# Decode attention: rotary keys gathered feature-first, and all scores of a half batch in one burst

## The chip, the cores and the metric

The kernel runs on one core of a Trainium2 chip. The metric is the device time of one execution in microseconds (us), lower is better. The kernel before takes 1249.53 us, the median of 3 runs (1249.14 to 1250.53). The engines are named as the profile names them: PE is TensorE's matmul (PEld its weight loads), DVE is VectorE, ACT is ScalarE, POOL is GpSimd, SP is SyncE, which here issues DMAs.

## The reference

One layer of a hybrid decoder is computed for a prompt of 512 tokens and for 8 sampled sequences of 4 tokens each, with shared weights in float32: a SwiGLU feed-forward network (FFN), a mixer of a gated linear recurrence (HGRN2) and latent attention (MLA) side by side, and a second FFN. The part that the change touches is the attention of the sampled tokens over their past of 4096 positions, which lie in a cache of pages of 128 rows, found through a page table:

```python
past_c = cache_kv_latent[l][page_table].reshape(Bs, past_len, KV_LORA)   # 256 latent features
past_r = cache_k_rope[l][page_table].reshape(Bs, past_len, QK_ROPE)      # 64 rotary features
...
s = (einsum('bqhr,bsr->bhqs', ql, c_kv) + einsum('bqhd,bsd->bhqs', qr, k_rope)) * scale
p = softmax(s, axis=-1)
return einsum('bhqs,bsr->bqhr', p, c_kv)
```

Each sequence has 4 tokens x 4 heads = 16 queries. A score is a product over 256 latent and 64 rotary features; the value product reads the same latent rows again. The host may lay out inputs beforehand; both kernels use that for weights, and the changed one for the rotary cache too.

## The kernel before, in words

The program is one stream of instructions written by Python and placed on the engines in an order that follows the source with small shifts. It has these stages: the first FFN over all tokens (to about 395 us in the profile), the recurrence, the prompt's attention with the output projection of the first half of the prompt, then the **decode stage** (`decode`, L1437), in which the attention of the sampled tokens over the cache runs interleaved with the second FFN of the first half of the prompt (`gb`, the generator `ffn`, L324), and at last the rest of that FFN and the second half of the tokens.

In the decode stage two generators are stepped in turn (L1517 to L1528): 94 steps of `decode`, with 100 steps of `gb` spread evenly among them. A step of `gb` is a few dozen FFN matmuls: gate and up products (L277) with their sigmoid work on ACT and DVE, or down products (L288 and L259). Their weights come by DMA from SP into `wraw`, and each tile is split in a rounded part `wh` on ACT (L250) and the rest `wl` on DVE (L251).

The past of a sequence is split in two halves of 2048 positions: 16 objects `Half` (L1352), each with two blocks of 1024 positions. A block is a tile of 128 partitions with 8 rows each.

- `gather` (L1360) fetches a block of latent rows (8 KB per partition) by an indirect DMA on POOL into one of seven slots (`ulb`, `uhb`, `ha`, `hb`, `mb`, `q0`, which the profile shows as `q`, and `dx`).
- `gather_r` (L1369) does the same for the rotary rows of both blocks of a half: two indirect DMAs of 2 KB per partition into `rraw`, which has two buffers.
- `turn` (L1376): scores need the features on the partitions. A DVE transpose of 32x32 blocks turns 64 features of a block into `kh`. A half takes five steps (`JS`, L65): the rotary features (8, 9) first, then the latent ones two by two; each step is two transposes of 128x512, one per block. `kh` has four buffers.
- `score` (L1384) multiplies a step's `kh` with the queries `qbd` on PE: 16 matmuls of 64 partitions x 32 queries x 128 positions, which run side by side on parts of the array (in the trace an instruction takes 269 ns and they start about 14 ns apart). The five steps accumulate in two PSUM banks. Which steps are multiplied where is set by `RUNS` (L68): steps 0 to 2 (48 matmuls) at step 2 of the five steps of a cycle, steps 3 and 4 (32 matmuls) at step 4. Then the scores are copied to SBUF (L1399, ACT and DVE) and their maximum is taken (L1401). `qsplit` (L1247) prepares the queries of the next sequence.
- `peak` (L1403), one cycle later: the maximum is spread with a matmul `pm` (L1405), reduced on DVE (L1407, L1410), the exponential is taken on ACT (L1411), transposed on DVE (`pt`, L1413) and copied into `pbuf` (L1417, 12 copies on ACT and 4 on DVE).
- `value` (L1419), at step 4 of that cycle and right behind the scores of the next half: 16 matmuls of `pbuf` with the latent blocks as they were gathered (L1426). Then the freed slots are gathered anew.

In the trace every float32 matmul stands as two instructions, so 48 matmuls are x96; a row of the instruction order counts matmuls.

The loop that sets this order:

```python
for st in range(len(JS)):
    if at(2):
        for k in RUNS.get(st, ()):
            at(2).score(k)
...
    if n > 1 or n == 1 and st >= 1:
        if n != 2 or st >= 2:
            turn(at(2).top if at(2) and st == len(JS) - 1 else None)
```

`at(k)` is the half whose gathers began k cycles ago, and `turn(top)` queues the next transpose on DVE, with `top` behind the maximum of the scores. The gather of the next half's rotary rows is issued with the first transpose of a half (L1452), once `rraw` has been turned.

## Time and profile before

| what | value |
|---|---|
| timed runs | 1249.14, 1249.53 and 1250.53 us, median 1249.53 |
| profiled execution, first to last instruction (span) | 1241.4 us |
| its mean granted TensorE clock | 0.999 |
| PE busy | 1215.0 us (98%) |
| DVE busy | 982.7 us (79%) |
| ACT busy | 738.8 us (60%) |
| POOL busy | 76.5 us (6%) |
| first score transpose to last value product of the stage | 707.3 to about 951 us |

The profiled execution has no other time than its span; 8.1 us lie between the span and the median of the timed runs. Busy time is the union of an engine's instructions, and the ends of matmuls are modelled, so PE can lose time between two starts without showing as idle. In a row of the timeline there stand the start, the length, the engine, the source line, the operation, the tile written and those read, the count, and in brackets the idle time of the engine before it and what ended that. In a row of the chain of waits there stand start, length, engine, tile and line.

### The profile page before, as it was taken

To read this page: it belongs to the slowest core of one execution; us is meant where nothing else is said; L and a number is where in the kernel's file an instruction comes from. 1 tells how busy PE (TensorE), PEld (TensorE's weight loads), DVE (VectorE), ACT (ScalarE), POOL (GpSimd) and SP (SyncE) were. 2 spreads that over 40 slices of the span, in tenths; PEclk is the share of its full clock that TensorE was granted. 3 is DMA by queue.
4 is the path that set the end of the run, shared out by engine and by line. 5 is a ranking of instruction groups with operands and counts; after the bars stand their busy time and mean duration, and the time that the engine had idled before them with its cause. 6 is when DMAs were issued, how large, how long until landed. Compare 5 with 4: busy or idle time off the path is not lost.

```text
span 1241.4 us, 29997 instructions
## 1 busy us (share of the span) xinstructions
PE 1215.0 (98%) x12366; PEld 1151.3 (93%) x12366; DVE 982.7 (79%) x1976; ACT 738.8 (60%) x1559; POOL 76.5 (6%) x80
## 2 busy tenths in 40 slices
PE   8999999999999999999999999999999999999997
PEld 6999999999999989988898888888888999999997
DVE  7897788878678888786877899999998778566665
ACT  7675545455366744545758766666656776554455
POOL 0000000000000000000001312322310000000000
PEclk9999999999999999999999999999999999999999
DMA  6232333232264213333233868878776635545451
GB/s 238 86 115 90 103 103 102 86 99 91 62 221 147 82 54 105 88 94 130 85 105 117 339 214 303 310 282 323 258 275 232 198 106 188 184 137 188 150 151 60
DMA packets 73113, 195.59 MB, mean 158 GB/s; under 512 B 12336, under 2 KB 27728, under 8 KB 68240
## 3 DMA queue, kind: packets, MB, share of 16 engines
q1 hardware_dynamic: 64512, 150.47, 37.3%
q0 software_dynamic: 7168, 41.95, 9.2%
q8 instruction: 97, 1.59, 0.5%
q10 hardware_dynamic: 1296, 1.26, 0.3%
q14 instruction: 40, 0.33, 0.1%
HBM read 183.97 MB, written 9.67 MB: 156 GB/s over the span
## 4 chain that ended last, share of the span: by engine, by line
PE 79%; DVE 11%; ACT 7%; issue 2%; DMA 2%; SPq 0%; DVEq 0%; ACTq 0%
PE acc L259 29%; PE acc L277 13%; PE dn L259 8%; PE Y L575 7%; PE X L575 4%; PE Z L575 4%; DVE kh L1381 3%; PE acc L731 3%; DVE wl L251 2%; ACT wh L250 1%; PE s L1393 1%; ACT pbuf L1417 1%; DMA wraw<-w_g 1%; PE pa L952 1%; PE o L1426 1%
## 5 line engine op out<-in xcount | busy, mean ns | idle before, releaser
L250 ACT CAST wh<-wraw 128x1024 fp32r<-128x1024 f32 (+2 forms) x194 | 185.0, 957 | 164.3 <-PE acc L259 103.7
L251 DVE TENSOR_TENSOR wl<-wraw,wh 128x1024 fp32r<-128x1024 f32 (+2 forms) x194 | 214.6, 1108 | 72.2 <-ACT wh L250 71.6
L277 PE MATMUL acc<-uha,wh 128*128 128x256 f32 (+1 forms) x528 | 155.5, 295 | 0.1
L277 PE MATMUL acc<-uha,wl 128*128 128x256 f32 (+1 forms) x528 | 150.0, 285 | 0.8 <-DVE wl L251 0.7
L277 PE MATMUL acc<-ula,wh 128*128 128x256 f32 (+1 forms) x528 | 150.5, 286 | 0.0
L259 PE MATMUL acc<-uhb,wh 128*128 128x288 f32 (+1 forms) x432 | 128.0, 296 | 0.0
L259 PE MATMUL acc<-uhb,wl 128*128 128x288 f32 (+1 forms) x432 | 127.0, 295 | 1.0 <-DVE wl L251 0.8
L259 PE MATMUL acc<-ulb,wh 128*128 128x288 f32 (+1 forms) x432 | 127.5, 295 | 0.0
L277 PEld LDWEIGHTS acc<-uha,wh 128*128 128x128 f32 x528 | 99.2, 188 | 8.8 <-issue 7.9
L277 PEld LDWEIGHTS acc<-uha,wl 128*128 128x128 f32 x528 | 99.2, 188 | 2.3 <-DVE wl L251 1.6
L277 PEld LDWEIGHTS acc<-ula,wh 128*128 128x128 f32 x528 | 99.4, 188 | 1.6 <-issue 1.2
L259 PEld LDWEIGHTS acc<-uhb,wl 128*128 128x128 f32 x432 | 81.2, 188 | 1.6 <-DVE wl L251 1.6
L259 PEld LDWEIGHTS acc<-uhb,wh 128*128 128x128 f32 x432 | 81.0, 187 | 0.2 <-ACT uhb L170 0.2
L259 PEld LDWEIGHTS acc<-ulb,wh 128*128 128x128 f32 x432 | 81.1, 188 | 0.1
L259 PE MATMUL dn<-hh,dh 128*128 128x272 f32 x256 | 74.3, 290 | 0.0
L259 PE MATMUL dn<-hh,dl 128*128 128x272 f32 x256 | 73.7, 288 | 0.0
L259 PE MATMUL dn<-hl,dh 128*128 128x272 f32 x256 | 73.6, 288 | 0.0
L277 PE MATMUL acc<-uhb,wh 128*128 128x272 f32 x176 | 52.8, 300 | 0.0
L1417 ACT COPY pbuf<-pt 32x64 f32<-32x64 f32 x192 | 46.5, 242 | 10.1 <-DVE pt L1413 7.3
L259 PE MATMUL acc<-hlb,wh 128*128 128x288 f32 x176 | 52.1, 298 | 0.0
L259 PE MATMUL acc<-hhb,wh 128*128 128x288 f32 x176 | 51.8, 298 | 0.0
L1393 PE MATMUL s<-kh,q 64*32 64x128 f32 x2560 | 48.0, 273 | 3.5 <-DVE kh L1381 3.5
(632 smaller groups left out, 3881.3 us busy)
## 6 DMA issues: line engine op xcount, KB each, us to landing
wraw<-w_u SPq DMA_DIRECT2D x66, 512.0 KB, 4.3
wraw<-w_g SPq DMA_DIRECT2D x65, 512.0 KB, 3.9
wraw<-w_d SPq DMA_DIRECT2D x40, 384.0 KB, 3.5
wraw<-w_in SPq DMA_DIRECT2D x24, 512.0 KB, 3.5
wraw<-w_d SPq DMA_DIRECT2D x32, 320.0 KB, 3.1
wraw<-w_d SPq DMA_DIRECT2D x16, 512.0 KB, 3.8
wraw<-w_o SPq DMA_DIRECT2D x16, 512.0 KB, 3.7
g_S<-state SPq DMA_DIRECT2D x4, 512.0 KB, 4.4
```

Source lines behind the costliest of these rows:

```text
L250: nc.scalar.copy(wh[:, :kt], w[:, :kt])
L251: nc.vector.tensor_tensor(wl[:, :kt], w[:, :kt], f32(wh[:, :kt]), op=ALU.subtract)
L259: nc.tensor.matmul(out, a, b, start=n == 0, stop=n == last)
L277: nc.tensor.matmul(acc[:, :n], a[:, k], b[:, k], start=k + i == 0, stop=k == kt - 1 and i == 2)
L575: nc.tensor.matmul(bank, a[p][:, k], b[q][:, k], start=first and k + n == 0, stop=k == 3 and n == 2, skip_group_check=True)
L731: nc.tensor.matmul(accs[x, d], wts[d][p][:, k], hs[k // 2][q][:, k % 2, x], start=k + n == 0, stop=k == nf - 1 and n == 2)
L952: nc.tensor.matmul(po[es, c].rearrange("p (n m) -> p n m", m=m), kx[:, cs], up(qx[:, cs], m), start=True, stop=True, skip_group_check=True)
L1381: nc.vector.transpose(kh[:, g].rearrange("p a j k -> p a (j k)"), src)
L1393: nc.tensor.matmul(self.s[r][c * 32 : c * 32 + 32, :P], q[rs, j], kh, start=st + jj == 0, stop=st == len(JS) - 1 and jj == 1, skip_group_c ...
L1417: (nc.scalar.copy if g else nc.vector.tensor_copy)(self.p[g * 32 : g * 32 + 32, c // 2, c % 2 * 4 : c % 2 * 4 + 4, self.i * 16 : self.i * ...
L1426: nc.tensor.matmul(o[g : g + 32, :R], self.p[:, c, a], self.craw[c][:, a], start=i + c == 0 and a < 4, stop=i + c == 2 and a >= 4, skip_gr ...
```

## The change

The rotary cache is laid out by the host so that, within a page, a feature's values for all positions lie together (features 0 to 31 as rows, and in each row the two halves of the features, the row number within the group of 8, and 16 positions). `gather_r` then brings rows that are already turned: four indirect DMAs of 1 KB per partition for a half, with an index tile `idr` of their own, into `rk` (two buffers, one per block). The five transposes of a half become four; a step of rotary scores reads `rk` directly, in runs of 16 values. The rotary features are now the last step.

`score` makes all 80 matmuls of a half at step 4 of the cycle (`RUN`), right ahead of the value products. `TURNS` sets two transposing steps at step 0 and one each at steps 1 and 2 of the same cycle; the first waits for the maximum of the scores before. The query split of the next sequence stands behind the maximum. The index tile takes two small loads on SP (`pr_sb`, `p32`) and one DVE operation in `decode_prep`. The numbers of steps of `decode` and `gb` stay 94 and 100.

```diff
-JS = ((8, 9), (0, 1), (2, 3), (4, 5), (6, 7))
+JS = ((0, 1), (2, 3), (4, 5), (6, 7), (8, 9))
 KHB = 4
-PEAK = 1
-RUNS = {2: (0, 1, 2), 4: (3, 4)}
+STEPS = 5
+PEAK, RUN = 1, 4
+TURNS = (2, 1, 1, 0, 0)
...
             def decode_prep():
+                pr_sb = mk([P, 2 * NBLK], I32, "pr_sb")
+                nc.sync.dma_start(pr_sb, ptr)
+                p32 = mk([P, 1], F32, "p32")
+                nc.sync.dma_start(p32, cf[:, C_P32 : C_P32 + 1])
+                nc.vector.tensor_scalar(out=idr, in0=pr_sb, scalar1=float(RD // 2), scalar2=p32, op0=ALU.mult, op1=ALU.add)
...
             def gather_r(self):
                 for blk in (2 * self.n, 2 * self.n + 1):
-                    rraw = mk([P, ROWS, RD], F32, "rraw", 2)
-                    off = bass.IndirectOffsetOnAxis(ap=idx[:, blk : blk + 1], axis=0)
-                    nc.gpsimd.indirect_dma_start(rraw.rearrange("p a r -> p (a r)"), None, pool_r, off)
-                    self.rraw.append(rraw)
+                    rk = mk([P, 2, 2, ROWS, 16], F32, "rk", 2)
+                    for i in range(2):
+                        off = bass.IndirectOffsetOnAxis(ap=idr[:, 2 * blk + i : 2 * blk + i + 1], axis=0)
+                        nc.gpsimd.indirect_dma_start(rk[:, i].rearrange("p j a k -> p (j a k)"), None, pool_r, off)
+                    self.rk.append(rk)
...
-            def score(self, st):
+            def score(self):
                 q = qbd[self.b % 2]
-                if st == 0:
-                    self.s = [ps("s", own=True) for _ in range(2)]
-                for jj, j in enumerate(JS[st]):
-                    for c in range(4):
-                        for r in range(2):
-                            rs = slice(r * 64, r * 64 + 64)
-                            kh = self.kh[st][rs, c // 2, c % 2 * 4 : c % 2 * 4 + 4, jj]
-                            nc.tensor.matmul(self.s[r][c * 32 : c * 32 + 32, :P], q[rs, j], kh, start=st + jj == 0, stop=st == len(JS) - 1 and jj == 1, skip_group_check=True)
-                if st == 1 and self.i and self.b + 1 < NB:
-                    qsplit(self.b + 1)
-                if st < len(JS) - 1:
-                    return
+                self.s = [ps("s", own=True) for _ in range(2)]
+                for st, js in enumerate(JS):
+                    for jj, j in enumerate(js):
+                        for c in range(4):
+                            for r in range(2):
+                                rs = slice(r * 64, r * 64 + 64)
+                                as_ = slice(c % 2 * 4, c % 2 * 4 + 4)
+                                if j < 8:
+                                    kh = self.kh[st][rs, c // 2, as_, jj]
+                                    out = self.s[r][c * 32 : c * 32 + 32, :P]
+                                else:
+                                    kh = self.rk[c // 2][rs, :, jj, as_].rearrange("p i a k -> p a i k")
+                                    out = self.s[r][c * 32 : c * 32 + 32, :P].rearrange("p (a i k) -> p a i k", a=4, i=2)
+                                nc.tensor.matmul(out, q[rs, j], kh, start=st + jj == 0, stop=st == len(JS) - 1 and jj == 1, skip_group_check=True)
...
                 self.top = nc.vector.tensor_reduce(self.mx, self.e, axis=AX.X, op=ALU.max)
+                if self.i and self.b + 1 < NB:
+                    qsplit(self.b + 1)
...
-            ups = [(h_, st) for h_ in H for st in range(len(JS))]
+            ups = [(h_, st) for h_ in H for st in range(len(JS) - 1)]
...
-                    if st == 0 and h_.n + 1 < NH2:
-                        H[h_.n + 1].gather_r()
...
-                for st in range(len(JS)):
-                    if at(2):
-                        for k in RUNS.get(st, ()):
-                            at(2).score(k)
+                for st in range(STEPS):
+                    if st == RUN and at(2):
+                        at(2).score()
                     if n < 3 and st == 0:
-                        if n == 0:
-                            H[0].gather_r()
                         gather(2 + n // 2)
+                    if st == 0 and 0 <= n - 1 < NH2:
+                        at(1).gather_r()
...
-                    if n > 1 or n == 1 and st >= 1:
-                        if n != 2 or st >= 2:
-                            turn(at(2).top if at(2) and st == len(JS) - 1 else None)
+                    if n > 1:
+                        for i in range(TURNS[st]):
+                            turn(at(3).top if at(3) and st + i == 0 else None)
...
-        "pool_r": g["cache_k_rope"].reshape(-1, ROWS * RD),
+        "pool_r": np.ascontiguousarray(g["cache_k_rope"].reshape(-1, 16, ROWS, 2, 32).transpose(0, 4, 3, 2, 1)).reshape(-1, 16 * ROWS * 2),
...
+        "ptr": np.ascontiguousarray(np.repeat(g["page_table"].reshape(NBLK, 4, 2), 32, axis=1).transpose(1, 0, 2)).reshape(P, 2 * NBLK),
```

## The prediction

> **What bounds the kernel now.** I read the slices of the page first, to find the stage that the change touches, then the busy time by stretches. Columns: stretch, length, then PE, weight loads (PEld), DVE, ACT and POOL busy with instruction counts, granted clock, DMA share, GB/s.

> ```profile
> 707.00:754.00 47.00, 44.65 (x777) 39.65 (x779) 45.85 (x97) 29.69 (x70) 8.97 (x9) 1.00 0.73 265
> 754.00:798.00 44.00, 44.00 (x803) 39.40 (x807) 39.85 (x84) 28.37 (x76) 13.28 (x12) 1.00 0.90 321
> 798.00:839.00 41.00, 39.58 (x802) 33.90 (x785) 38.87 (x89) 26.46 (x74) 12.81 (x12) 1.00 0.77 270
> 839.00:884.00 45.00, 44.86 (x848) 40.10 (x854) 43.02 (x94) 27.25 (x72) 11.98 (x12) 1.00 0.86 313
> 884.00:941.00 57.00, 56.56 (x1114) 48.87 (x1100) 52.98 (x121) 35.00 (x97) 11.91 (x11) 1.00 0.69 241
> 941.00:1241.00 300.00, 290.78 (x2222) 285.67 (x2214) 202.39 (x337) 177.41 (x322) 1.35 (x1) 0.99 0.51 159
> ```

> The decode stage is the first five rows, 234 us. TensorE is busy 229.65 of them and VectorE 220.57 (the sums of their columns): two engines stand close to full, so PE time saved counts only while DVE follows. The clock is full and DMA is not the limit except for stretches at 0.90. The last row is untouched by the change.

> Next, the chain of waits through that stage, in order of time (start, length, what).

> ```profile
> 752.61 0.68 DVE kh L1381
> 753.33 0.64 PE s L1393 x24
> 753.97 1.86 PE o L1426 x32
> ...
> 794.53 3.04 PE acc L277 x24
> ...
> 848.90 1.52 PE s L1393 x96
> 850.42 4.46 PE acc L259 x36
> 854.88 1.09 PE s L1393 x64
> 855.97 1.86 PE o L1426 x32
> ```

> PE alternates between FFN pieces and two score bursts per half batch, and in places a score burst stands behind a DVE transpose (first two rows). Each matmul counts as two instructions here: 48 score matmuls are x96, 32 are x64. The waits of the stage (total us, times, longest):

> ```profile
> POOL rraw L1373 <- DVE kh L1381: 133.3, 16, 13.3
> ...
> PEld s L1393 <- DVE kh L1381: 5.4, 7, 1.7
> ...
> PE s L1393 <- DVE kh L1381: 3.5, 7, 1.4
> ```

> What one such wait looks like on PE:

> ```profile
> 836.77 0.67 PE L1393 MATMUL s<-kh,q 64*32 64x128 f32 x32
> 838.54 0.42 PE L1393 MATMUL s<-kh,q 64*32 64x128 f32 x8 [1.11 <-DVE kh L1381]
> 839.14 0.64 PE L1393 MATMUL s<-kh,q 64*32 64x128 f32 x24 [0.17 <-DVE kh L1381]
> 839.71 1.07 PE L1426 MATMUL o<-ulb,pbuf 128*32 128x256 f32 x16
> ```

> The x64 burst takes 839.71 - 836.77 = 2.94 us instead of 1.09: 1.85 lost, of which 1.28 show as PE idle. So the 3.5 us of idle understate the loss; the 5.4 us of the weight loads are nearer, since 3.5 x 1.85/1.28 = 5.1.

> **The change, part by part.** *Bursts merged.* From the chain: 32 more score instructions cost 1.52 - 1.09 = 0.43 us, 0.0134 each; one burst of 160 would take 1.09 + 96 x 0.0134 = 2.38 us where the two take 2.61: 0.23 saved. An FFN piece costs (4.46 - 3.04)/12 = 0.118 us per matmul, so x24 holds 3.04 - 24 x 0.118 = 0.20 us that does not scale, paid at each break; one break less saves it. Together 0.43 us of pure PE time per half batch. The first of the 16 halves is broken up otherwise, so 15 x 0.43 = 6.5 us, on the path as long as PE is.

> *Score waits on transposes.* Now all transposes of a half are queued early in its cycle and the burst stands at its end, so the 5.4 us should go. Bounds: 3.5 (PE's idle alone) and 8.9 (both rows added, as if they never overlapped).

> *Rotary transposes removed.*

> ```profile
> L1381 DVE STREAM_TRANSPOSE kh<-rraw 128x512 f32<-128x512 f32 x32 | 20.4, 675 | 0.0
> ```

> 20.4 us of DVE work go, 1.3 per half. PE hides them except for the waits already counted, so they are worth nothing by themselves; they give DVE room to keep up with a PE that is 4% faster: 220.57 - 20.4 = 200.2 us in about 224, 89%.

> *What comes next: softmax to value.* In gate/up halves the value products stand right behind another chain, shown for one half, from the end of its scores (first row) to its value products (last):

> ```profile
> 810.84 0.64 PE L1393 MATMUL s<-kh,q 64*32 64x128 f32 x24 [0.28 <-DVE kh L1381]
> ...
> 815.04 0.42 DVE L1401 TENSOR_REDUCE mxh<-q 128x1 f32<-128x256 f32 x1
> ...
> 819.30 1.18 DVE L251 TENSOR_TENSOR wl<-wraw,wh 128x1024 fp32r<-128x1024 f32 x1
> ...
> 820.74 0.28 DVE L1407 TENSOR_REDUCE q<-pm 128x16 f32<-128x128 f32 x1
> ...
> 821.34 0.51 ACT L1411 ACTIVATE q<-q,mbd 128x256 f32<-128x256 f32 x1 [1.18 <-DVE mq L1410]
> ...
> 822.63 0.44 DVE L1413 STREAM_TRANSPOSE pt<-q 128x256 f32<-128x256 f32 x1
> ...
> 823.27 3.07 ACT L1417 COPY pbuf<-pt 32x64 f32<-32x64 f32 x12
> ...
> 825.27 1.29 DVE L1381 STREAM_TRANSPOSE kh<-rraw 128x512 f32<-128x512 f32 x2
> ...
> 825.67 1.07 PE L1426 MATMUL o<-q,pbuf 128*32 128x256 f32 x16
> ```

> Probabilities are complete at 823.27 + 3.07 = 826.34, 0.7 us after the value products began (these need the last of them only in their second half). So this chain, 14.9 us from the scores' end at 811.48, has no slack today. It is made of DVE queueing: 3.6 us until the maximum starts, 7.6 from there to the transpose `pt`. In the changed order two transposes (0.6 us each by the spacing of such rows) come ahead of `pt` and two weight subtractions (about 1.15 each, the 819.30 row) go behind it: 1.1 us less; and 1.3 us per half less queue ahead of the maximum. I take 12 to 12.5 us. It stands against cycles, from one half's value products to the next, of 11.8 (the shortest I find, 14.04 us between the 825.67 and 839.71 rows less 1.85 of wait and 0.43) to 13.8 (811.48 to 825.67 less 0.43): a wait of under 1 us in some halves, 1.0 us in all; bounds 0 and 5.4, all that the other wait gave.

> *Rotary gathers.* 64 of them replace 32, and with two buffers those of the next half can only start when the burst has read the last; a latent gather queues behind four instead of two.

> ```profile
> 811.65 0.95 POOL L1373 DMA_INDIRECT rraw<-pool_r,idx  x1 [7.29 <-DVE kh L1381]
> 812.90 0.95 POOL L1373 DMA_INDIRECT rraw<-pool_r,idx  x1 [0.30 <-issue]
> 814.16 0.95 POOL L1366 DMA_INDIRECT hb<-pool_c,idx  x1 [0.31 <-issue]
> ...
> 827.50 1.51 POOL L1373 DMA_INDIRECT rraw<-pool_r,idx  x1 [0.30 <-issue]
> ```

> Their landing (minimum, median, maximum from issue), first of `rraw`, then of the latent gathers, in this stage:

> ```profile
> DMA to landing us min/median/max: 3.3/4.6/6.8
> ```

> ```profile
> DMA to landing us min/median/max: 6.2/8.5/10.9
> ```

> Pitch 1.25 us. The fourth rotary gather starts 0.2 + 3 x 1.25 = 4.0 us after the burst and lands at 7.3 to 10.8; the next burst reaches its rotary part 0.45 us before its end (32 instructions), at 11.8 - 0.45 = 11.3 or later. Covered. The latent gather starts at 811.65 + 5.0 = 816.65 instead of 814.16. Its first reader in this case:

> ```profile
> 830.12 0.67 DVE L1381 STREAM_TRANSPOSE kh<-hb 128x512 f32<-128x512 f32 x1
> ```

> Today 830.12 - 814.16 - 8.5 = 7.5 us of slack. Of that 2.5 go to the queue and 2 to 4 to the shorter cycle and the earlier maximum: 1 to 3 are left at the median landing, none at 10.9. A late one stops DVE and all behind it, the softmax chain above first. I charge 0.5 us, bounds 0 and 4. Bytes are the same, so the DMA share rises only by the shorter stage.

> *Rotary scores.* 16 of the 80 matmuls read runs of 16 floats instead of 32. No row shows such a read. Nearest are the `kh` rows at 0.0134 us per instruction; the other end is twice that, 32 x 0.0134 = 0.43 us per half, 6.9 in all. I take 0, since the element count is the same. [...] No trace of before can show it.

> *Small edits.* Two small loads on SP and one DVE operation of 64 elements ahead of the stage: 0.2 us, bounds 0 and 4.6 if DVE had to wait for a landing. The query split moves behind the maximum; its copies are the same: 0.

> How the order moves. PE, one half in the gate/up part, `s` scores, `o` value products, `acc` FFN. Before:

> ```order
> L277 MATMUL acc<-ula,wh 128x256
> L277 MATMUL acc<-uha,wl 128x256
> L1393 MATMUL s<-kh,q_8192 32x128 x32
> L1426 MATMUL o<-q_8787,pbuf 32x256 x8
> L1426 MATMUL o<-dx,pbuf 32x256 x8
> L277 MATMUL acc<-uha,wh 128x256
> ```

> and now:

> ```order
> L280 MATMUL acc<-uha,wl 128x256
> L1409 MATMUL s<-kh,q_8193 32x128 x64
> L1409 MATMUL s<-rk,q_8193 32x128 x16
> L1440 MATMUL o<-q_8793,pbuf 32x256 x8
> L1440 MATMUL o<-dx,pbuf 32x256 x8
> L280 MATMUL acc<-uha,wh 128x256
> ```

> The 48 that stood alone in the FFN are now in front of the value products. DVE at the end of the same half, `pt` to the copy of the next scores. Before:

> ```order
> L1413 STREAM_TRANSPOSE pt<-q_8192 128x256
> L1381 STREAM_TRANSPOSE kh<-ulb 128x512
> L1417 COPY pbuf<-pt 32x4x16 x4
> L1381 STREAM_TRANSPOSE kh<-uhb 128x512
> L336 TENSOR_TENSOR sil<-sil,sit 128x256
> L1381 STREAM_TRANSPOSE kh<-rraw 128x512 x2
> L365 TENSOR_TENSOR sil<-sil,acc 128x256
> L251 TENSOR_TENSOR wl<-wraw,wh 128x768
> ```

> and now:

> ```order
> L1427 STREAM_TRANSPOSE pt<-q_8193 128x256
> L254 TENSOR_TENSOR wl<-wraw,wh 128x1024
> L1431 COPY pbuf<-pt 32x4x16 x4
> L254 TENSOR_TENSOR wl<-wraw,wh 128x1024
> L254 TENSOR_TENSOR wl<-wraw,wh 128x768
> L339 TENSOR_TENSOR sil<-sil,sit 128x256
> ```

> No transpose for the scores stands behind `pt` any more; weight work has moved there. POOL in the same part, `rraw` and `rk` rotary gathers, the rest latent ones. Before:

> ```order
> L1373 DMA rraw<-pool_r,idx 128x512 x2
> L1366 DMA hb<-pool_c,idx 128x2048
> L1366 DMA mb<-pool_c,idx 128x2048
> L1373 DMA rraw<-pool_r,idx 128x512 x2
> L1366 DMA q_8787<-pool_c,idx 128x2048
> ```

> and now:

> ```order
> L1383 DMA rk<-pool_r,idr 128x256 x4
> L1375 DMA hb<-pool_c,idx 128x2048
> L1375 DMA mb<-pool_c,idx 128x2048
> L1383 DMA rk<-pool_r,idr 128x256 x4
> L1375 DMA q_8793<-pool_c,idx 128x2048
> ```

> The latent gathers keep their places, each pair behind four.

> **The sum.** The profiled span is 1241.4 us, the median of the timed runs 1249.5; I keep the 8.1 us between them. -6.5 (bursts) -5.4 (waits) +1.0 (softmax) +0.5 (gathers) +0.2 = -10.2: **1239.3 us**, a span near 1231.

> **Rivals.**
> *Softmax takes the place of the transposes.* PE gets faster, the value products wait for `pbuf`, and the 5.4 us come back there. For: no slack today. Against: DVE loses 1.3 us per half on that very chain. 1249.5 - 6.5 + 0 to 2: 1243 to 1245.
> *Short runs at half pace.* The 6.9 us are paid on PE: 1239.3 + 6.9 = 1246.2. Against: the same number of elements.
> *Slower: the rotary gather becomes the cycle.* Burst end, four gathers, landing, burst: if the fourth landed later than about 9.4 us from its issue (past about 10.1 the whole gain is gone), a cycle of 13.8 us (102.0 us for 7 halves between the 753.97 and 855.97 rows, less 0.43 and 0.36 of waits) could not hold it (13.8 - 0.45 - 4.0). At the latent gathers' worst, 10.9, each half loses 1.5 us more, 22 in all: 1239.3 + 22 = 1261. For: four in a row cannot be started ahead. Against: 6.8 at worst today, 2.6 short of the point. [...]
> *More.* The start of the stage, where the scores stood in five pieces, gives 2 to 4 us more: 1236. That the change doesn't do what it says is excluded by the order.

> **Chances.** The forecast 0.60 (its own range 1236.5 to 1242); more 0.05; softmax 0.18; half pace 0.09; gather 0.08. A measurement of this kernel tells about 0.2%, 2.5 us, from no change. Faster: 0.60 + 0.05 + 0.18 + a third of half pace 0.03 = 0.86; same: the rest of half pace, 0.06; slower 0.08. The range leaves out half pace, the gather case and the tip of "more", 0.20 in all: 1234.5 to 1245.

> **What would show it.** Right: 160 score instructions in one piece of about 2.4 us without a break, PE not waiting for `kh`, no `kh<-rraw`, DVE about 200 us in a stage of about 224. Wrong: value products (`o`) or DVE transposes that wait (for `pbuf`, for a latent gather), a break inside the burst ahead of `rk`, or the last x32 of a burst longer than 0.43 us.

## The result, and the profile after

| | median | runs | against before in the same sitting |
|---|---|---|---|
| new kernel | 1261.38 us | 1254.59 to 1267.29 (6) | before 1250.36 us; ratio 1.0084, interval 1.0060 to 1.0108 |
| new kernel, once more (e14) | 1262.68 us | 1260.66 to 1265.76 (4) | before 1250.03 us; ratio 1.0099, interval 1.0077 to 1.0122 |

The kernel is slower by 0.8 to 1.0%, some 11 us, where 1239.3 us (0.8% faster) was forecast. The result lies outside the range and on the other side.

First the same stretches of the profile after as were read before (columns as there):

```profile
754.00:798.00 44.00, 40.69 (x678) 37.40 (x679) 34.15 (x75) 24.89 (x68) 15.34 (x16) 0.96 0.86 304
798.00:839.00 41.00, 36.40 (x723) 31.45 (x707) 33.60 (x76) 23.97 (x66) 18.44 (x18) 0.96 0.75 253
```

VectorE is down as forecast (34.15 us where it was 39.85), but TensorE is no longer full: 40.69 of 44 us and 36.40 of 41, with 678 matmuls where there were 803. The clock is 0.96 instead of 1.00. The last value products of the stage tell where the loss lies. They start here in the new kernel:

```profile
965.95 1.41 PE L1440 MATMUL o<-hb,pbuf 128*32 128x256 f32 x16
```

and here in the kernel before:

```profile
950.17 1.41 PE L1426 MATMUL o<-hb,pbuf 128*32 128x256 f32 x16
```

That is 15.8 us later, and the spans of the two profiles differ by 1257.5 - 1241.4 = 16.1: all of it is in the decode stage. The medians differ by 11.0 us only, since the first profile of before is of a quicker execution than its timed runs (e12 below). What TensorE waits for there (total us, times, longest):

```profile
PEld o L1440 <- issue: 12.9, 17, 3.0
...
PE o L1440 <- issue: 7.9, 5, 2.5
...
PEld o L1440 <- ACT pbuf L1431: 6.8, 11, 1.5
...
PEld s L1409 <- issue: 4.5, 2, 2.3
...
PE s L1409 <- issue: 4.0, 2, 2.0
```

No row has a wait of the scores for `kh` any more: that part came as forecast. In its place stand long waits with "issue", which means that the profile shows nothing that was waited for. Two of them in the timeline of TensorE, and between them a score burst that runs through to its value products (that half breaks one value product later, at 802.65; the view starts at 781, so its first row lacks the burst's first 8 instructions):

```profile
780.77 1.90 PE L1409 MATMUL s<-kh,q 64*32 64x128 f32 x120
782.41 0.76 PE L1409 MATMUL s<-rk,q 64*32 64x128 f32 x32
783.10 1.07 PE L1440 MATMUL o<-dx,pbuf 128*32 128x256 f32 x16
783.99 0.61 PE L1440 MATMUL o<-ulb,pbuf 128*32 128x256 f32 x7
787.07 0.95 PE L1440 MATMUL o<-ulb,pbuf 128*32 128x256 f32 x9 [2.47 <-issue]
...
797.31 2.03 PE L1409 MATMUL s<-kh,q 64*32 64x128 f32 x128
799.08 0.74 PE L1409 MATMUL s<-rk,q 64*32 64x128 f32 x32
799.76 1.07 PE L1440 MATMUL o<-uhb,pbuf 128*32 128x256 f32 x16
...
827.98 0.74 PE L1409 MATMUL s<-rk,q 64*32 64x128 f32 x31
830.67 0.29 PE L1409 MATMUL s<-rk,q 64*32 64x128 f32 x1 [1.95 <-issue]
```

The two breaks come in the midst of a row of equal matmuls, whose operands the ones before had read already. The page's list of DMA queues has one that led on:

```profile
q8 instruction: 97, 1.59, 0.5%
```

97 packets of 16 KB, 1.59 MB. The trace has 24,964 instructions of TensorE, counting the weight load of each matmul (a score burst of 160 and the 32 value products behind it make 384, in 2.45 us, from 797.31 to 799.76, and 1.86 us). 1.59 MB over 24,964 are 64 bytes each, so a packet holds 256, and 97.5 such blocks fit the 97 packets; in e8 below, 2048 more instructions bring 8 more packets. So I counted the place of each break among TensorE's instructions in the trace, and took from the trace when the last packet before it had landed. These are all breaks over 1.4 us in the stage, from the start of the matmul before (time of the end in us, length, place among TensorE's instructions, place modulo 256, time since the last packet landed):

```
787.07  2.85  14530  194  1.39
802.65  2.01  15042  194  1.35
830.67  2.22  16066  194  1.50
846.34  2.27  16577  193  1.42
940.41  1.46  19906  194  1.41
955.34  2.25  20418  194  1.43
```

Every one falls on the same place modulo 256 (which place it is depends on where the count starts), and ends 1.35 to 1.50 us after a packet has landed. This looks as if TensorE had used up its instructions; e2, e3 and e8 test it.

### The profile page after: what moved, and what is told of

It reads as the page before. It is cut to its first block, busy times and chain, and to the rows that moved or that the text cites. A ratio compares the mean times of both kernels' runs of the same rounds, so it can differ in the third digit from the quotient of the medians.

```text
span 1257.5 us, 30075 instructions
## 1 busy us (share of the span) xinstructions
PE 1217.1 (97%) x12366; PEld 1155.1 (92%) x12366; DVE 965.2 (77%) x1945; ACT 739.1 (59%) x1559; POOL 105.2 (8%) x112
## 3 DMA queue, kind: packets, MB, share of 16 engines
q8 instruction: 97, 1.59, 0.5%
## 4 chain that ended last, share of the span: by engine, by line
PE 85%; ACT 7%; DVE 5%; issue 2%; DMA 0%; SPq 0%; DVEq 0%; another core or an unknown queue 0%; ACTq 0%
PE acc L262 30%; PE acc L280 17%; PE dn L262 8%; PE Y L578 6%; PE X L578 4%; PE Z L578 4%; PE acc L734 3%; PE s L1409 2%; PE o L1440 2%; ACT wh L253 2%; DVE kh L1391 1%; ACT pbuf L1431 1%; PE pa L956 1%; PE s L1206 1%; DVE wl L254 1%
## 5 line engine op out<-in xcount | busy, mean ns | idle before, releaser
L254 DVE TENSOR_TENSOR wl<-wraw,wh 128x1024 fp32r<-128x1024 f32 (+2 forms) x194 | 214.8, 1110 | 81.6 <-ACT wh L253 75.7
L280 PE MATMUL acc<-uha,wh 128*128 128x256 f32 (+1 forms) x528 | 155.5, 295 | 0.7 <-issue 0.7
L280 PE MATMUL acc<-ula,wh 128*128 128x256 f32 (+1 forms) x528 | 151.8, 288 | 0.0
L280 PE MATMUL acc<-uha,wl 128*128 128x256 f32 (+1 forms) x528 | 151.3, 287 | 0.3 <-issue 0.2
L280 PEld LDWEIGHTS acc<-uha,wh 128*128 128x128 f32 x528 | 100.5, 191 | 8.2 <-issue 7.6
L280 PEld LDWEIGHTS acc<-ula,wh 128*128 128x128 f32 x528 | 100.6, 191 | 1.5 <-issue 1.2
L280 PEld LDWEIGHTS acc<-uha,wl 128*128 128x128 f32 x528 | 100.5, 190 | 1.5 <-issue 0.9
L1383 POOL DMA_INDIRECT rk<-pool_r,idr x64 | 67.2, 1051 | 147.5 <-PE s L1409 124.5
L280 PE MATMUL acc<-uhb,wh 128*128 128x272 f32 x176 | 52.8, 300 | 0.0
L262 PE MATMUL acc<-hhb,wl 128*128 128x288 f32 x176 | 51.4, 294 | 0.0
```

Of the source, the lines that this page charges most:

```text
L254: nc.vector.tensor_tensor(wl[:, :kt], w[:, :kt], f32(wh[:, :kt]), op=ALU.subtract)
L262: nc.tensor.matmul(out, a, b, start=n == 0, stop=n == last)
L280: nc.tensor.matmul(acc[:, :n], a[:, k], b[:, k], start=k + i == 0, stop=k == kt - 1 and i == 2)
L1383: nc.gpsimd.indirect_dma_start(rk[:, i].rearrange("p j a k -> p (j a k)"), None, pool_r, off)
```

## The experiments

Three theories were tested. **F** (fetch): TensorE's instructions come in blocks of 256. The next block is there 4 to 6 us after the current one is entered (in the six rows above 4.0 to 5.7 us lie between the entry and the end of the break), and the joined run of 384 dense instructions uses one up faster (384 in 2.45 + 1.86 us, so 256 in some 2.9). **G**: the rotary gathers. First meant as gathers or rotary rows that come late; after e1 as G2: many gathers in a row disturb TensorE. **S**: the value products wait for the probabilities.

The runs fell on several chips, on which the kernel before takes 1250 to 1252 us, and on one (e9, e10) 1244; so ratios to before in the same sitting are compared. A ratio to before still holds what the two gathers of before cost on that chip: e1 to e4 ran on one chip, e5 to e8 on a second, e9 and e10 on a third, e11 to e14 on a fourth. The table has each run's ratio with its interval. Then follow, worked out from the starts of successive matmuls in the decode stage, the time over a bound (0.03 us in scores, 0.07 in value products, 0.215 in FFN, where the usual spacing is 0.014, 0.06 on average and 0.12): at block boundaries (place 190 to 197 modulo 256), elsewhere in scores and elsewhere in FFN. These sums move by up to about 1 us with the bound. The column "half clock" is the time in the stage with a granted clock of 0.50. The last column is the time from the first score matmul to the last value product. The 3.6 us in scores of the kernel before are its waits for `kh`.

| run | ratio (interval) | boundary | scores | FFN | half clock | stage |
|---|---|---|---|---|---|---|
| before, first profile | 1 | 3.2 | 3.6 | 0 | 0 | 239.5 |
| before, e12 | 1 (1250.44 us, one run) | 2.8 | 8.2 | 0 | 0 | 246.2 |
| new, first profile | 1.0084 (1.0060-1.0108) | 15.3 | 0 | 4.8 | 6.8 | 254.9 |
| new, e14 | 1.0099 (1.0077-1.0122) | 15.2 | 0 | 8.5 | 10.2 | 258.8 |
| e1 new, cut burst | 1.0156 (1.0131-1.0182) | 5.3 | 8.1 | 12.7 | 6.8 | 266.0 |
| e2 new, 64 more instructions | 1.0158 (1.0131-1.0185) | 21.4 | 0 | 8.3 | 17.1 | 266.8 |
| e3 new, 192 more | 1.0099 (1.0063-1.0136) | 12.6 | 0 | 4.6 | 6.8 | 255.2 |
| e4 new, no rotary gather | 0.9990 (0.9978-1.0002) | 10.6 | 0 | 1.9 | 0 | 242.5 |
| e5 before, four rotary gathers | 1.0259 (1.0240-1.0278) | 2.2 | 24.4 | 1.6 | 17.1 | 281.0 |
| e6 cut burst, no rotary gather | 0.9930 (0.9911-0.9950) | 3.3 | 2.3 | 0 | 0 | 238.8 |
| e7 before, no rotary gather | 0.9933 (0.9915-0.9951) | 3.0 | 3.9 | 0 | 0 | 239.6 |
| e9 new, half the rotary gathers | 1.0037 (1.0023-1.0050) | 13.9 | 0 | 1.5 | 0 | 246.0 |
| e10 before, one rotary gather | 0.9991 (0.9982-1.0000) | 2.6 | 4.3 | 0 | 0 | 237.9 |
| e11 cut burst, four gathers of 32 bytes | 1.0184 (1.0145-1.0222) | 3.9 | 8.2 | 5.9 | 10.2 | 262.0 |
| e13 as e10, other chip | 0.9935 (0.9919-0.9952) | 3.2 | 4.0 | 0 | 0 | 238.6 |

**e2 and e3: instructions in front.** 16 or 48 one-column matmuls (64 or 192 instructions) in TensorE's idle first microseconds; nothing else changes.

```diff
+    pz = pp.tile([P, 512], F32, name="pz", tag="pm", bufs=1)
+    for _ in range(16):
+        nc.tensor.matmul(pz[:32, :1], ones[:64, :32], ones[:64, :1], start=True, stop=True, skip_group_check=True)
```

> The new kernel with 64 more TensorE instructions (16 matmuls of one column) in its first, idle 5 us; every later instruction stands 64 further on in its block. Theory F: the breaks move to where the block boundary now falls, each 64 instructions earlier in the program: halves of the down projections that had none (868 to 900 us) get breaks of 1 to 3 us, and every break still ends at the same place modulo 256, about 1.4 us after a 16 KB instruction packet has landed. In sum 0 to 7 us more: 1261 to 1268. Theories G and S: the breaks stay at the same instructions and sizes, time within 0.4% of the new kernel's 1261.4.

> As with 64, but 192 more. Theory F: halves whose boundary fell in the burst's first third (those of 787 to 846 us) now have it in the middle and lose most of their breaks; breaks appear in the halves around 868 to 900 us and at the start of the stage (750 to 775 us). In sum 0 to 6 us less: 1254 to 1262. Theories G and S: the same breaks as in the new kernel, within 0.4% of 1261.4.

Measured: 1271.37 us and 1262.14 us. The breaks moved, and in both every break over 2 us stands again at place 193 or 194 modulo 256. With 64 more, value products break in a half that had run through in the new kernel, where it reads:

```profile
880.69 1.07 PE L1440 MATMUL o<-mb,pbuf 128*32 128x256 f32 x16
881.58 1.05 PE L1440 MATMUL o<-q,pbuf 128*32 128x256 f32 x16
```

and here, in e2:

```profile
889.25 1.07 PE L1443 MATMUL o<-mb,pbuf 128*32 128x256 f32 x16
890.13 0.61 PE L1443 MATMUL o<-q,pbuf 128*32 128x256 f32 x8
893.72 0.64 PE L1443 MATMUL o<-q,pbuf 128*32 128x256 f32 x8 [2.97 <-issue]
```

That is place 17,858, 194 modulo 256. With 192 more, the breaks at 787 to 816 us are gone and others stand at 741, 757, 849 and 864. Seven to ten microseconds (by the ratios of e14 and of the first runs) from 64 idle instructions: F is shown, and neither G nor S can move a break so. Which halves lose changes, though; that some do does not, since a cycle is 514 to 584 instructions and the place drifts. In time, e2 was over its 1261 to 1268, and e3 0.1 us over the 1254 to 1262 of its range.

**e8: a dense run by itself.** 512 score-shaped matmuls at the start of the kernel before, where no gather runs.

```diff
...
+    for n in range(512):
+        c, r = n // 2 % 4, n % 2
+        rs = slice(r * 64, r * 64 + 64)
+        nc.tensor.matmul(pz[r][c * 32 : c * 32 + 32, :P], ones[rs, :32], ones[rs], start=n < 8, stop=n >= 504, skip_group_check=True)
```

> The kernel before with 512 more score-shaped matmuls (2048 TensorE instructions, 8 blocks) in one run at its start, where no gather runs; their result is read by nobody. Theory F: each block of 256 instructions is used up in 1.9 us and then TensorE waits for the next until 3 to 5 us after it entered the last: 8 blocks in 24 to 40 us, breaks 256 instructions apart, each ending 1.4 us after a 16 KB packet has landed. Otherwise: 2048 x 0.0075 = 15 us without a break.

Measured: 35 us for the run, from 1.05 to 36.1. TensorE in order of time:

```profile
1.05 5.33 PE L421 MATMUL pz<-ones 64*32 64x128 f32 x223 [1.05 <-DVE epst L423]
8.97 3.43 PE L421 MATMUL pz<-ones 64*32 64x128 f32 x128 [2.59 <-issue]
15.16 3.48 PE L421 MATMUL pz<-ones 64*32 64x128 f32 x128 [2.77 <-issue]
21.09 2.69 PE L421 MATMUL pz<-ones 64*32 64x128 f32 x128 [2.44 <-issue]
24.82 5.99 PE L421 MATMUL pz<-ones 64*32 64x128 f32 x256 [1.03 <-issue]
32.00 2.02 PE L421 MATMUL pz<-ones 64*32 64x128 f32 x128 [1.19 <-issue]
35.45 0.70 PE L421 MATMUL pz<-ones 64*32 64x128 f32 x33 [1.44 <-issue]
```

From the first break on, they stand 128 of these rows, that is 256 instructions with the weight loads, apart (the x256 row hides one of 0.5 us at 28.54; the two rows of over 3.4 us ran at a granted clock of 0.50). From resumption to resumption it is 6.2 us at first (8.97 to 15.16) and 3.45 at the end (32.00 to 35.45), where the work of the block takes 2.02. So F holds without any gather, and it has a size: in a long dense run a block of 256 takes TensorE some 3.5 us or more. A single dense block can be quicker. In the new kernel the blocks entered at 735.40, 747.15 and 859.74 us are through in 2.0 to 2.4 us without a break; in each case the transfer of two packets, not one, had begun while the long block before was worked off. F's "4 to 6 us" is thus no constant, and a break also depends on how long the block before took.

**e1: the burst cut.** 48 score matmuls two steps earlier, 32 with the value products; gathers and layout stay new.

```diff
...
-                    if st == RUN and at(2):
-                        at(2).score()
+                    if st in (2, RUN) and at(2):
+                        at(2).score(st // RUN)
```

> The new kernel with its score burst cut as before: 48 score matmuls two steps ahead, 32 (the rotary ones among them) joined to the value products; rotary layout, gathers and transposes stay as in the new kernel. Theory F (fetch): TensorE's instructions arrive in blocks of 256, the next one 4 to 5.7 us after the current one is entered; the joined run of 384 instructions uses one up in 2.9 us, the cut one (192, then 128 + 64) never does, so the 8 breaks of 1.1 to 2.9 us (15.5 us) go. Burst merging then gives nothing, the score waits still give: 1249.5 - 5.4 + 1.5, 1244 to 1249. Theory G (rotary gathers, or latent gathers behind four, are late): nothing of that changes, 1257 to 1265. Theory S (value products wait for probabilities): the chain is the same length and the cycle too, 1255 to 1262.

Measured: 1270.27 us. Outside what each theory had. The boundary breaks fell from 15.3 to 5.3 us, as F says, but there are 20.8 us of other breaks, where the new kernel had 4.8:

```profile
PEld acc L280 <- issue: 11.9, 32, 1.1
PEld s L1410 <- issue: 11.1, 15, 2.3
...
PE s L1410 <- issue: 9.3, 11, 2.1
...
PE acc L280 <- issue: 4.8, 9, 0.8
```

These keep to no place in a block. TensorE does a few matmuls, stops, does a few more, mostly in steps of 0.7 to 1.4 us, and it does so while GpSimd issues gathers or within 2 us of it. F alone falls with this run; G2 comes from it.

**e4: no rotary gather.** Halves 1 to 15 read half 0's rows; the rest of the rotary keys is left out.

```diff
...
+                if self.n:
+                    self.rk = first[0].rk
+                    return
+                first.append(self)
```

> The new kernel without the rotary gathers of halves 1 to 15: every half reads half 0's rotary keys (this part of the computation is left out). Theory G: no gather to wait for, latent gathers are issued 5 us earlier: the 12 us against before and part of the forecast gain come back, 1240 to 1250. Theory F: breaks and times as in the new kernel, but for 8 MB less traffic: 1254 to 1263, breaks ending at the same block boundaries. Theory S: as F in time.

Measured: 1249.09 us. 1.0084 - 0.9990 is 0.94%, 11.7 us, that the four rotary gathers cost the new kernel. The boundary breaks stayed at their places (786.52 and 944.34 us among them) but shrank to 10.6: without the gathers the packets come a little sooner, too (from the entry into a block to the start of the next packet 1.8 us in the median, 2.4 in the new kernel).

**e6 and e7: no rotary gather, cut burst and kernel before.** The same edit on e1 and on the kernel before, which leaves out the same.

> The cut burst (48, then 32 joined to the value products) without the rotary gathers of halves 1 to 15 (left out: each half reads half 0's rotary keys). Theory F: the breaks at block boundaries, 10.6 us in the run without rotary gathers and the joined burst, fall to about 3 as before; the 6.5 us of merging are given back: 1245 to 1250. Theory G2: no run of more than two gathers, so none of the breaks that made the cut kernel 1270: 20 us under it. If the cut itself were what costs, it would stay at 1260 or more.

> Control: the kernel before without the rotary gathers of halves 1 to 15 (left out). Theory G2: runs of four gathers cost little there, so 0 to 3 us less than before: 1247 to 1250. If any rotary gather costs what the four of the new kernel do, half of their 12 us: 1244.

Measured: 1242.98 and 1243.60 us. e4 against e6 differs in the joining alone (and in the chip): the medians are 6.1 us apart, the ratios 0.9990 - 0.9930, 0.6% or 7.5 us. So the joining costs more than it saves. In the two profiles the stage is 3.7 us longer with the burst joined: the boundary breaks take 10.6 - 3.3 = 7.3 us more, and about 4 of that come back, since there are fewer changes between scores and FFN. e6 against e7, on one chip, differs in the rotary transposes and in what part of the score waits goes with them, first e6:

```profile
PE s L1416 <- DVE kh L1397: 1.2, 4, 0.5
```

then e7:

```profile
PE s L1399 <- DVE kh L1387: 3.5, 7, 1.4
```

The ratios are 0.9930 and 0.9933. The 20.4 us of transposes and what of the waits goes in e6 were worth nothing that shows.

**e5: before with six gathers.** Each rotary gather cut into two halves: with the two latent ones, six gathers for a half batch where before has four.

```diff
...
+                    for i in range(2):
+                        off = bass.IndirectOffsetOnAxis(ap=id2[:, blk, i : i + 1], axis=0)
+                        nc.gpsimd.indirect_dma_start(rraw[:, 4 * i : 4 * i + 4].rearrange("p a r -> p (a r)"), None, pool_r, off)
```

> The kernel before, with each of its two rotary gathers per half batch cut into two of half the size: six gathers in a row on GpSimd instead of four, the same bytes to the same place, the same order of all else (two burst pieces, transposes as before). Theory G2 (five or six gathers in a row slow the whole core: TensorE then runs a few matmuls at a time in steps of 0.7 or 1.4 us with nothing to wait for, and its instruction packets come later): breaks of that kind appear 4 to 6 us after a run of gathers has begun, 0.5 to 1.5 us per half: 1256 to 1264. Theory F alone (instruction blocks, only the dense run matters): no run of TensorE is denser than before: 1249 to 1252.

Measured: 1284.72 us, 32 us over before and above the range of G2. One burst beside its gathers, both engines by time:

```profile
739.53 0.95 POOL L1377 DMA_INDIRECT rraw<-pool_r,id  x1 [10.62 <-DVE kh L1385]
...
740.27 1.00 PE L1397 MATMUL s<-kh,q 64*32 64x128 f32 x44
...
740.78 1.00 POOL L1377 DMA_INDIRECT rraw<-pool_r,id  x1 [0.30 <-issue]
...
742.08 1.20 POOL L1377 DMA_INDIRECT rraw<-pool_r,id  x1 [0.30 <-issue]
...
742.34 0.44 PE L1397 MATMUL s<-kh,q 64*32 64x128 f32 x5 [0.38 <-issue]
...
743.10 0.45 PE L1397 MATMUL s<-kh,q 64*32 64x128 f32 x4 [0.32 <-issue]
...
743.59 0.46 DVE L171 TENSOR_TENSOR hla<-sil,hha 128x256 fp32r<-128x256 f32 x1
...
743.59 0.95 POOL L1377 DMA_INDIRECT rraw<-pool_r,id  x1 [0.30 <-issue]
...
743.87 0.42 PE L1397 MATMUL s<-kh,q 64*32 64x128 f32 x4 [0.32 <-issue]
```

44 score instructions in the first 1.3 us, then at most 5 every 0.75 us, until 1.8 us after the last gather's start. VectorE works on beside it until it has to wait for the scores. The bytes are the same as before; the number of gathers does this.

**e9: half the rotary gathers in the new kernel.** One page of each pair is read and stands for both, so half of the rotary keys are left out.

```diff
-                    for i in range(2):
+                    for i in range(2 if self.n < 1 else 1):
...
```

> The new kernel with two rotary gathers per half batch instead of four (one page of each pair is read and stands for both; half of the rotary keys are left out), same rows of 256 floats, joined burst. Theory G2 (the number of gathers in a row counts): runs of four as before, so most of the 12 us that no rotary gather gave: 1249 to 1254, with the breaks at instruction blocks left (10 to 13 us). If the short rows themselves count, half of it: 1255 to 1257.

Measured: 1249.43 us beside 1244.21 for before, on the chip where before is fastest. But for one wait of 1.3 us for a weight tile (`wl`), no breaks but the boundary ones are left (13.9 us), and it is still 0.37% slower: the joined burst's cost on a chip where one gather less per half gives the kernel before 0.9 us (e10 below). What two gathers less are worth can't be read here, since the new kernel with four never ran on this chip.

**e11: four gathers of 32 bytes.** e1 without the rotary bytes (all halves use half 0's keys, the rest is left out), but with as many gathers, and four matmuls of one column per half that read them.

```diff
...
+                for i in range(4):
+                    rx = mk([P, 8], F32, "rx", 4)
...
+                    nc.gpsimd.indirect_dma_start(rx, None, pool_r.rearrange("n (a b) -> (n a) b", b=8), off)
```

> The cut burst of e1 with half 0's rotary keys for all (left out: the rest), and, where e1 has its four rotary gathers, four gathers of 32 bytes per row: the same number of gathers, rows and places in GpSimd's order, a 32nd of the bytes. If the issuing counts (instructions, descriptors): the breaks in steps of 0.7 us are there as in e1, ratio to before 1.010 to 1.018. If the bytes count: as without rotary gathers, 0.993 to 0.996.

Measured: 1270.47 us, ratio 1.0184 (1.0145 to 1.0222), as e1 with all its bytes. The waits are those of e1 too:

```profile
PEld acc L280 <- issue: 11.5, 30, 1.0
PEld s L1422 <- issue: 11.4, 16, 2.2
```

The issuing counts, not the bytes. Every gather here has 128 rows, one to a partition, so whether it is the gathers or their rows that count is not told apart.

**e10 and e13: one rotary gather.** The kernel before with 16 tokens to a row, so that one gather serves a half; the cache layout, the index and the order in which the scores read `kh` change with it.

```diff
-                for blk in (2 * self.n, 2 * self.n + 1):
-                    rraw = mk([P, ROWS, RD], F32, "rraw", 2)
-                    off = bass.IndirectOffsetOnAxis(ap=idx[:, blk : blk + 1], axis=0)
-                    nc.gpsimd.indirect_dma_start(rraw.rearrange("p a r -> p (a r)"), None, pool_r, off)
+                rraw = mk([P, 2, ROWS, RD], F32, "rraw")
+                off = bass.IndirectOffsetOnAxis(ap=idr[:, self.n : self.n + 1], axis=0)
+                nc.gpsimd.indirect_dma_start(rraw.rearrange("p u a r -> p (u a r)"), None, pool_r, off)
...
```

> The kernel before with one rotary gather per half batch instead of two: pages spread over 8 partitions and rows of 16 tokens, the cache laid out so that the rows are whole; the same bytes, the same transposes and order. Theory G2: runs of three gathers instead of four; no rotary gather at all gave 7 to 8 us, so half of that: 1244 to 1248, faster than both kernels. Otherwise 1249 to 1252.

> The kernel before with one rotary gather per half (e10), timed once more. Theory G2, where before stands at 1250 or more: 0.993 to 0.998 of before. Where before stands at 1244: again 0.999.

Measured: 1243.29 us where before is at 1244.21 (ratio 0.9991), and 1242.12 us where it is at 1250.03 (ratio 0.9935). On the second chip it is faster than both kernels, by 0.65% than the one before. On the first there was next to nothing to gain.

**e12 and e14: both kernels again, on the chip of e13.**

> The kernel before, unchanged, for its profile on this chip. Its first profile has a span 8.1 us under the median of its times; the runs since have 1.8 us between span and time. If that profile was of a chip on which the gathers do not disturb TensorE, this one, at 1250 to 1253, has 6 us of breaks in steps of 0.7 us in score bursts that stand beside rotary gathers, and its stage is 246 us long instead of 239.5; at 1244 it has none.

> The new kernel, unchanged. Where before stands at 1250 or more: 1.006 to 1.011 of it, breaks at block boundaries 12 to 16 us. Where before stands at 1244, the breaks in steps of 0.7 us are gone but those at the boundaries stay: 1.005 to 1.010.

Measured: 1250.44 and 1262.68 us. In the kernel before, two gathers already disturb a score burst, in the same steps:

```profile
915.30 0.92 PE L1393 MATMUL s<-kh,q 64*32 64x128 f32 x47
...
915.89 0.95 POOL L1373 DMA_INDIRECT rraw<-pool_r,idx  x1 [7.89 <-DVE kh L1381]
...
916.45 0.42 PE L1393 MATMUL s<-kh,q 64*32 64x128 f32 x3 [0.23 <-issue]
...
917.15 0.95 POOL L1373 DMA_INDIRECT rraw<-pool_r,idx  x1 [0.30 <-DVE wl L251]
...
917.18 0.43 PE L1393 MATMUL s<-kh,q 64*32 64x128 f32 x5 [0.31 <-issue]
...
917.93 0.41 PE L1393 MATMUL s<-kh,q 64*32 64x128 f32 x4 [0.33 <-issue]
...
918.65 0.44 PE L1393 MATMUL s<-kh,q 64*32 64x128 f32 x5 [0.31 <-issue]
```

Its last value products start at 957.33 here, 7.2 us after the 950.17 of the first profile. That profile had none of this.

## Why the prediction was wrong, point by point

*Bursts merged, -6.5.* This step failed. The burst itself is what was forecast: 2.45 us from its first score to the value products (797.31 to 799.76 in the new profile; 2.38 forecast). But "0.43 us of pure PE time per half batch" took it that TensorE gets its instructions as fast as it can execute them. Joined to the value products, the burst outruns the fetch, and what the merging saves is more than given back: some 4 us are saved, but the breaks at block boundaries take 7.3 us more in e4 than in e6 and 12.4 more in e14 than in e12. e4 against e6 says 6 to 7.5 us slower by joining, not 6.5 faster.

*Score waits, -5.4.* The waits went, all of them, in the new kernel. Their price was too high or is given back elsewhere; which of the two is open. e6, with 1.2 us of TensorE idle for `kh` where e7 has 3.5, is not measurably faster than it.

*Rotary transposes.* 20.4 us of VectorE's work worth nothing by itself: right.

*Softmax to value, +1.0.* About right. The 6.8 us of weight loads waiting for `pbuf` (1.9 before) show on TensorE as under 1 us with that name, and a break of 1.17 at 908.40 that stands beside the last probability copies. S is not the cause: e6 has the same chain and 238.8 us.

*Gathers, +0.5 (0 to 4).* The second step that failed, and by itself enough to lose the forecast gain. All that was reckoned was when a gather lands and who waits for it, and that held: no score burst waits for `rk`, and a rotary gather still occupies GpSimd for 0.95 us (median of 58). Not reckoned was what issuing it does to TensorE: 11.7 us in the joined burst (e4), 28 in the cut one (1.0156 - 0.9930, e1 and e6, on two chips), 32 for two more in the kernel before (e5).

*Short runs, 0.* Right: the 32 rotary scores of the burst at 799.08 take 0.68 us to the first value product; less the 0.20 us that the change from scores to value products takes (its median in both profiles), 0.015 each, against 0.014 for the others (1.77 us for 128).

*The 8.1 us between span and time.* Kept as a constant, wrongly. In the later runs 1.7 to 2.3 us lie between. By that, the profile worked from was of an execution that took about 1243 us; of the rest, 6.7 us are in the decode stage itself (239.5 us there, 246.2 in e12), mostly as breaks in score bursts beside gathers.

*The rivals.* "The rotary gather becomes the cycle" gives 1261 us, the time that was measured, by a mechanism that is not there: it asked for landings past 9.4 us, and e11 shows that the same loss comes with 32 bytes a row. It was right that four gathers in a row are the trouble, and wrong in how.

On one chip, e14 against e12: boundary +12.4, FFN breaks +8.5, breaks and waits in scores -8.2, and some 4 us lost in 10.2 us at half clock (FFN matmuls start 0.215 us apart there instead of 0.12), 17 in sum; the stage is 12.6 longer. The 4 us between are what fewer changes from piece to piece give, the part of the merging that did come.

What stays open: by which way the issue of gathers stops TensorE, why one chip shows nothing of it with two, and why the cost grows faster than the number. The runs show that it is not the bytes, not the place in an instruction block and not a landing that is waited for; whether the gathers or their rows count, they do not show.

## What to carry to other kernels

Count instructions per microsecond as well as microseconds: here runs of 384 TensorE instructions, weight loads counted, which take 4.31 us unbroken, stalled at block boundaries for up to 2.85 us (first profile of the new kernel), so small matmuls were better kept between large ones than gathered in one burst (e6 0.9930, e4 0.9990). Count gathers by number, not by bytes (e11, with a 32nd of the rotary bytes of e1, stands at 1.0184, e1 at 1.0156): a cache layout that saves VectorE's work and doubles the gathers is a bad bargain, and one that makes a row twice as long, so that one gather does for two, gained 0.65% on one chip and 0.1% on another. And where the profiled span and the median of the times differ by more than the usual (8.1 us, where 1.8 was the rule), the missing time may lie in the very stage under study.

## What the runs showed of the hardware

A break can cost twice. After the one that ends at 787.07 in the new kernel the granted clock (third number from the right) is half for 3.4 us:

```profile
787.70:791.10 3.40, 3.40 (x19) 3.16 (x16) 1.06 (x2) 0.37 (x1) 2.24 (x3) 0.50 0.65 190
```

It followed an idle time of 2.47 us. The clock is half from 832.03 to 835.43 us too, after an idle time of 1.95 us before 830.67, while the idle times of 1.63 us before 802.65 and of 2.00 us before 846.34 had no such effect (clock 1.00 in the 3.4 us behind each). The length of the idle time alone does not tell these apart. In e5 a row of six pauses of 0.3 to 0.5 us, from 741.6 to 745.3 us, was followed by half clock too (745.9 to 749.4).

While GpSimd issues indirect DMAs, or within 2 us of it, TensorE stops in steps of 0.7 to 1.4 us in e1 and of some 0.75 us in e5 and e12; in e5 VectorE goes on beside it. The first profile of the kernel before has none of this. One rotary gather per half costs nothing that shows beside none (e13 0.9935, e7 0.9933, on two chips); two cost about 8 us on two chips (e7, e13) and some 1 us on another (e10), four 12 to 28 in the new layout, by what TensorE is doing, and in the kernel before (e5) 32 more than two.
